# Splitting a two-key one-hot comparison into two operations with different layouts, in a PEER channel mixer

## The chip, the cores and the metric

The kernel runs on one core of one Trainium2 chip. The metric is the device time of one execution in microseconds; a kernel's time is the median of its runs.

## The reference

The reference is two layers of a diffusion backbone over 512 latent tokens and 256 context tokens, model width 1024. Each layer has a token mixer (global attention in layer 0, windowed attention in layer 1) and then a PEER channel mixer, which is where the change is:

```python
q = (hb @ w_q).reshape(n, PEER_HEADS, PEER_QDIM)          # 8 heads, 256
s1 = jnp.einsum('nhd,kd->nhk', q1, sub_keys[0])           # 128 first keys
s2 = jnp.einsum('nhd,kd->nhk', q2, sub_keys[1])           # 128 second keys
v1, i1 = lax.top_k(s1, PEER_TOPK)                         # 16 each
v2, i2 = lax.top_k(s2, PEER_TOPK)
cand_s = v1[..., :, None] + v2[..., None, :]
cand_i = i1[..., :, None] * N_KEYS + i2[..., None, :]
top_s, pos = lax.top_k(cand_s, PEER_TOPK)
expert = jnp.take_along_axis(cand_i, pos, axis=-1)        # one of 128 x 128 experts
g = jax.nn.softmax(top_s, axis=-1)
act = jax.nn.gelu(jnp.einsum('nhkd,nd->nhk', u_tab[expert], hb))
out = jnp.einsum('nhk,nhkd->nd', g * act, v_tab[expert])
```

So each token picks 8 x 16 = 128 experts, each named by a first key (0 to 127) and a second key (0 to 127), and gives each a gate `g`.

## The kernel before, in words

Two of the six 128-token tiles of layer 0, and one of the four of layer 1, gather the rows of their experts (`sparse_gen`, by indirect transfers that GpSimd issues). The other tiles, four latent tiles in layer 0 and three in layer 1, are computed densely: `dense` (L639) multiplies the tokens with all 16384 experts and weights the activations by a gate matrix that is zero wherever an expert was not picked. It goes through the first keys in order; five of them are worked ahead (`LEAD`), and from then on the loop alternates `outputs` and `weights`.

The gate matrix is made per tile by `build_g` (L526), which is called from the main loop (L825) right behind `topk_scan` and `topk_resolve` (L822, L823) of the same tile. `topk_resolve` leaves in a PSUM bank, for each token (on the free axis) and each of its 128 picks (on the partitions), the first key, the second key and the gate. L530 casts the two keys to bf16 into `ib` (128 x 2 x 128 tokens), L532 copies the gates into `gt`.

`build_g` then takes the 128 tokens of the tile in 16 groups of eight (`TB`), inside four blocks of 32 (`GB`). For a group:

- L551, VectorE: one comparison of `ib` with a table `iota_t` (made at L104 by GpSimd; it holds the key number, repeated eight times along the token axis) gives `hot`, bf16, for both keys at once. Its layout is (key kind, key 0 to 127, token 0 to 7): the token is innermost.
- L554, VectorE: `first` = the first key's half of `hot` times the gate, f32, in the layout (token, key). The read of `hot` is therefore stepped by eight elements, and the gate is repeated along the key axis.
- L557, ScalarE: `second` = the second key's half of `hot`, cast to f32 in the layout (token, key), with the same stepped read.
- L562, TensorE: for each token one matmul of `second` with `first` over the 128 picks gives that token's 128 x 128 gate matrix in PSUM (`gm`), four tokens to a bank.
- L541: the banks are copied to `gsb`, three of four by ScalarE, one by VectorE, one half group behind the matmuls (`LAG`). When 32 tokens are complete, a 2 MB transfer on SP's queue writes them to `Gd` in DRAM (L543, issued through the helper at L154). `dense` reads `Gd` back as `Gt`, which it waits for.

`hot` has two buffers, by alternating tags, one of each; `first`, `second` and `gsb` have two each.

Beside `build_g` other work is in the engines' queues: the modulation weights of layer 1 in three of layer 0's tiles (`ada_load` and `ada_cols`, L828), and the first `weights` of `dense` (L168 to L170, with ScalarE's cast at L160 and VectorE's subtraction at L162). The order within each engine's queue is set when the kernel is built, by a scheduler that goes by the order of the source as priority and by when an operation's inputs are ready in its own model; so independent operations can be moved past each other. In the trace of before, the comparisons of two groups stand next to each other ahead of the two `first`.

L488, L492, L506 and L507, which the prediction uses for durations, are small steps of `topk_resolve`: L492 multiplies the gates with a per-head factor that is repeated along the innermost axis, L506 combines two contiguous operands of the same size, and L507 reads what L506 wrote.

Of the kernel before, what the change touches and what calls it, by code (L numbers as in the profile page):

```python
# [12 lines left out]
BF16 = mybir.dt.bfloat16  # L13
U32 = mybir.dt.uint32
AF = mybir.ActivationFunctionType
ALU = mybir.AluOpType
# [4 lines left out]
P = 128  # L21
# [13 lines left out]
NK = 128  # L35
# [7 lines left out]
TB = 8  # L43
# [26 lines left out]
def body(ctx, tc, xT_in, cT_in, ada_w, ada_b, gains1, gains2, w_qkv, qk_gain, w_o, sinks,  # L70
         w_pq, subk, u_t, u_n, v_b, v_n, ropeC, ropeS, ropeR, out):
    nc = tc.nc
    V, A, G, T = nc.vector, nc.scalar, nc.gpsimd, nc.tensor

    const = ctx.enter_context(tc.tile_pool(name="const", bufs=1))
# [5 lines left out]
    def bank(tag, name, bufs):  # L81
        return ps.tile([P, 512], F32, tag=tag, name=name, bufs=bufs)
# [19 lines left out]
    V.memset(epst, EPS)  # L102
    iota_t = const.tile([P, NK, TB], BF16, name="iota_t")
    G.iota(iota_t, [[1, NK], [0, TB]], channel_multiplier=0, allow_small_or_imprecise_dtypes=True)  # L104
    ind = const.tile([P, NH + NKV, 16], F32, name="ind")
    V.memset(ind, 0.0)
    for h in range(NH + NKV):
# [41 lines left out]
    def nm(s):  # L149
        uid[0] += 1  # L150
        return f"{s}_{uid[0]}"

    def dma(dst, src):
        nc.sync.dma_start(dst, src)  # L154
# [371 lines left out]
    def build_g(pt, Gd, t, gp, kp):  # L526


        ib = gp.tile([P, 2, P], BF16, tag="ib", name=nm("ib"), bufs=2)
        A.copy(ib.rearrange("p a b -> p (a b)"), pt[:, :2 * P])  # L530
        gt = gp.tile([P, P], F32, tag="gt", name=nm("gt"), bufs=2)
        A.copy(gt, pt[:, 2 * P:3 * P])  # L532
        HT = TB // 2
        pending = []
        count = [0]

        def evacuate():
            po, gs, o, b = pending.pop(0)
            count[0] += 1
            eng = V.tensor_copy if count[0] % 4 == 0 else A.copy  # L540
            eng(gs[:, :, o:o + HT], po.rearrange("p (t a) -> p a t", t=HT))  # L541
            if o + HT == GB:
                dma(Gd[:, :, t * (P // GB) + b].rearrange("s p f -> p s f"),  # L543
                    gs.rearrange("p (s a) t -> p s (a t)", a=SC))

        for b in range(P // GB):
            gs = gp.tile([P, NK, GB], F32, tag="gsb", name=nm("gsb"), bufs=GSB)
            for n8 in range(GB // TB):
                tok = slice(b * GB + n8 * TB, b * GB + (n8 + 1) * TB)
                hot = kp.tile([P, 2, NK, TB], BF16, tag=("hot", "rep")[n8 % 2], name=nm("hot"), bufs=1)  # L550
                V.tensor_tensor(hot, iota_t[:, None].to_broadcast([P, 2, NK, TB]),  # L551
                                ib[:, :, None, tok].to_broadcast([P, 2, NK, TB]), ALU.is_equal)
                first = gp.tile([P, TB, NK], F32, tag="first", name=nm("first"), bufs=2)
                V.tensor_tensor(first, hot[:, 0].rearrange("p a t -> p t a"),  # L554
                                gt[:, tok, None].to_broadcast([P, TB, NK]), ALU.mult)
                second = gp.tile([P, TB, NK], F32, tag="second", name=nm("second"), bufs=2)
                A.copy(second, hot[:, 1].rearrange("p a t -> p t a"))  # L557
                for half in range(2):
                    po = bank("bg", nm("gm"), 4)
                    for i in range(HT):  # L560
                        k = half * HT + i
                        T.matmul(po[:, i * P:(i + 1) * P], second[:, k], first[:, k], start=True, stop=True)  # L562
                    pending.append((po, gs, (n8 * 2 + half) * HT, b))
                    if len(pending) > LAG:
                        evacuate()
        while pending:
            evacuate()
# [168 lines left out]
    for L in range(DEPTH):  # L736
# [83 lines left out]
        with pool(f"gp{L}") as gp:  # L820
            for t in range(c0 // P, NLAT // P):
                topk_scan(tk["l", t], v12["l", t], 1, kt)  # L822
                pt = topk_resolve(tk["l", t], i12["l", t], kt, "bg", lambda i, shape: kt.tile(  # L823
                    shape, BF16, tag=("hot", "rep")[i], name=nm("hot"), bufs=1))
                build_g(pt, Gd, t - c0 // P, gp, kt)  # L825
                if not last:
                    if t < 3:
                        ada_cols(1, mods[1], t, wp, ada_load(1, t, wp, 0))  # L828
# [4 lines left out]
        with pool(f"db{L}") as db:  # L833
            rb = rb_es.enter_context(pool(f"rb{L}", right=True))
            sg = groups[-1]["nm"]
            with pool(f"kc{L}") as kc:
                prep = []
                for t in stiles:
                    with later(SLACK2):
                        for hb in range(2):  # L840
                            topk_scan(tk[sg, t], v12[sg, t], hb, kc)
                        pt = topk_resolve(tk[sg, t], i12[sg, t], kc, "O", lambda i, shape: rb.tile(
                            shape, BF16, tag=("gu", "gv")[i], name=nm("hot"), bufs=(GUB, GVB)[i]))
# [90 lines left out]
```

## Time and profile before

| what | value |
|---|---|
| median of 3 runs | 4043.28 us (4041.41 to 4055.09) |
| the profiled execution | 4048.38 us, its span 4046.6 us |
| busy over the span: TensorE, its weight loads | 93%, 79% |
| busy over the span: VectorE, ScalarE, GpSimd | 76%, 38%, 25% |

The profiled execution is one run of the program with the hardware profiler on. Its span runs from the first to the last instruction; what lies around it makes up the rest of that run's own time. Shares of busy time are means over the span, and the stages have different limits, so the part of the span in which an edit lies has to be read by itself.

### The profile page before, as it was taken

To read this page: it belongs to the slowest core of one execution; us is meant where nothing else is said; L and a number is where in the kernel's file an instruction comes from. 1 tells how busy PE (TensorE), PEld (TensorE's weight loads), DVE (VectorE), ACT (ScalarE), POOL (GpSimd) and SP (SyncE) were. 2 spreads that over 40 slices of the span, in tenths; PEclk is the share of its full clock that TensorE was granted. 3 is DMA by queue.
4 is the path that set the end of the run, shared out by engine and by line. 5 is a ranking of instruction groups with operands and counts; after the bars stand their busy time and mean duration, and the time that the engine had idled before them with its cause. 6 is when DMAs were issued, how large, how long until landed. Compare 5 with 4: busy or idle time off the path is not lost.

```text
span 4046.6 us, 52056 instructions
## 1 busy us (share of the span) xinstructions
PE 3753.2 (93%) x19384; PEld 3200.5 (79%) x19384; DVE 3091.0 (76%) x5913; ACT 1536.2 (38%) x2217; POOL 1000.8 (25%) x778
## 2 busy tenths in 40 slices
PE   7999897768999999999999999998679999999999
PEld 5767685657877777787777867767678999999999
DVE  3373799986888888888888755579997877778775
ACT  3262316863222222222222233534873333333332
POOL 0000000001444554444454300000002444444420
PEclk9999998989999999999999999999999999999999
DMA  4303128665898899988888721121567888888874
GB/s 176 125 1 115 58 67 268 188 188 174 297 322 316 310 320 329 324 312 317 316 317 319 250 87 52 45 77 46 154 209 245 303 301 297 296 297 297 305 261 157
DMA packets 343407, 894.08 MB, mean 221 GB/s; under 512 B 25968, under 2 KB 145904, under 8 KB 338800
## 3 DMA queue, kind: packets, MB, share of 16 engines
q1 hardware_dynamic: 232560, 488.05, 35.2%
q0 software_dynamic: 110592, 402.70, 28.6%
q8 instruction: 152, 2.49, 0.2%
q14 instruction: 103, 0.84, 0.1%
HBM read 826.16 MB, written 64.49 MB: 220 GB/s over the span
## 4 chain that ended last, share of the span: by engine, by line
PE 49%; issue 19%; DVE 13%; DMA 10%; POOL 8%; ACT 2%; POOLq 0%; SPq 0%; DVEq 0%; ACTq 0%
PE sp L170 5%; DMA gv<-v_n,idx 5%; PE sp L168 5%; PE sp L169 5%; DVE first L554 4%; POOL gv L598 4%; POOL gu L598 4%; PE pj L168 4%; PE pj L169 4%; PE pj L170 4%; DMA gu<-u_n,idx 3%; PE kp L682 2%; PE kp L683 2%; PE kp L681 2%; PE op L683 2%
## 5 line engine op out<-in xcount | busy, mean ns | idle before, releaser
L598 POOL DMA_INDIRECT gu<-u_n,idx x384 | 548.8, 1429 | 2670.0 <-DVE idx L578 964.3
L168 PE MATMUL sp<-hil,Uh 128*128 128x512 f32 (+1 forms) x2048 | 750.8, 367 | 29.8 <-ACT act L659 29.5
L169 PE MATMUL sp<-lol,Uh 128*128 128x512 f32 (+1 forms) x2048 | 751.2, 367 | 0.0
L170 PE MATMUL sp<-hil,Ul 128*128 128x512 f32 (+1 forms) x2048 | 747.0, 365 | 2.6 <-DVE Ul L162 2.6
L626 DVE SCALAR_TENSOR_TENSOR acc<-gv,w,acc 128x1024 f32<-128x1024 f32 x381 | 489.5, 1285 | 138.3 <-DMA gv<-v_n,idx 137.6
L667 ACT CAST wh<-act 128x512 fp32r<-128x512 f32 (+1 forms) x256 | 145.0, 567 | 1039.9 <-DVE act L665 1033.3
L598 POOL DMA_INDIRECT gv<-v_n,idx x384 | 448.9, 1169 | 330.8 <-DVE acc L626 220.2
L616 DVE CUSTOM_DVE_ANT_0 gu<-gu,hn 128x1024 f32<-128x1024 f32 x384 | 468.0, 1219 | 66.7 <-DMA gu<-u_n,idx 66.6
L168 PEld LDWEIGHTS sp<-hil,Uh 128*128 128x128 f32 x2048 | 387.4, 189 | 75.9 <-ACT act L659 30.2
L162 DVE TENSOR_TENSOR Ul<-Ur,Uh 128x1024 fp32r<-128x1024 f32 x256 | 312.4, 1221 | 170.8 <-ACT Uh L160 170.7
L682 PE MATMUL kp<-wh,Vl 128*128 128x512 f32 (+1 forms) x1024 | 381.9, 373 | 47.5 <-DVE Vl L162 47.2
L170 PEld LDWEIGHTS sp<-hil,Ul 128*128 128x128 f32 x2048 | 387.3, 189 | 47.1 <-DVE Ul L162 3.9
L169 PEld LDWEIGHTS sp<-lol,Uh 128*128 128x128 f32 x2048 | 387.6, 189 | 38.5
L160 ACT CAST Uh<-Ur 128x1024 fp32r<-128x1024 f32 x256 | 269.0, 1051 | 391.2 <-PE sp L169 384.5
L681 PE MATMUL kp<-wh,Vh 128*128 128x512 f32 (+1 forms) x1024 | 378.5, 370 | 0.8 <-ACT wh L667 0.7
L683 PE MATMUL kp<-wl,Vh 128*128 128x512 f32 (+1 forms) x1024 | 379.1, 370 | 0.0
L681 PE MATMUL op<-wh,Vh 128*128 128x512 f32 (+1 forms) x1024 | 371.3, 363 | 0.6 <-DVE xl L652 0.6
L683 PE MATMUL op<-wl,Vh 128*128 128x512 f32 (+1 forms) x1024 | 370.8, 362 | 0.0
L682 PE MATMUL op<-wh,Vl 128*128 128x512 f32 (+1 forms) x1024 | 370.7, 362 | 0.0
L160 ACT CAST Vh<-Vr 128x1024 fp32r<-128x1024 f32 x256 | 268.7, 1050 | 221.0 <-PE op L683 201.8
L562 PE MATMUL gm<-first,second 128*128 128x128 f32 x1792 | 239.9, 292 | 98.0 <-DVE first L554 88.1
L562 PEld LDWEIGHTS gm<-first,second 128*128 128x128 f32 x1792 | 223.9, 204 | 126.8 <-ACT second L557 79.3
(228 smaller groups left out, 6660.3 us busy)
## 6 DMA issues: line engine op xcount, KB each, us to landing
Ur<-u_t SPq DMA_DIRECT2D x256, 512.0 KB, 6.0
Vr<-v_b SPq DMA_DIRECT2D x256, 512.0 KB, 6.8
Gd<-gsb SPq DMA_DIRECT2D x28, 2048.0 KB, 9.1
Gt<-Gd SPq DMA_DIRECT2D x32, 1024.0 KB, 8.1
Gt<-Gd SPq DMA_DIRECT2D x32, 768.0 KB, 7.1
ar<-ada_w SPq DMA_DIRECT2D x32, 512.0 KB, 10.3
wr<-ada_w SPq DMA_DIRECT2D x32, 512.0 KB, 4.6
wr<-w_pq SPq DMA_DIRECT2D x32, 512.0 KB, 3.5
```

The costliest lines, as they stand in the source:

```text
L160: A.copy(hi, raw)
L162: V.tensor_tensor(lo, raw, hi, ALU.subtract)
L168: T.matmul(o, sh, mh, start=i == 0, stop=False)
L169: T.matmul(o, sh, ml, start=False, stop=False)
L170: T.matmul(o, sl, mh, start=False, stop=i == n - 1)
L562: T.matmul(po[:, i * P:(i + 1) * P], second[:, k], first[:, k], start=True, stop=True)
L598: G.indirect_dma_start(out=r, out_offset=None, in_=tab, in_offset=bass.IndirectOffsetOnAxis(ap=idx[:, s:s + 1], axis=0))
L616: V.tensor_tensor_reduce(out=r, in0=r, in1=hn, scale=1.0, scalar=0.0, op0=ALU.mult, op1=ALU.add, accum_out=sd[:, k:k + 1])
L626: V.scalar_tensor_tensor(acc[ti], r, w[:, k:k + 1], acc[ti], ALU.mult, ALU.add)
L681: T.matmul(o[:, :n], vh[:, k, ds], wh, start=start, stop=False, skip_group_check=True)
L682: T.matmul(o[:, :n], vl[:, k, ds], wh, start=False, stop=False, skip_group_check=True)
L683: T.matmul(o[:, :n], vh[:, k, ds], wl, start=False, stop=stop, skip_group_check=True)
```

## The change

The comparison of L551 becomes two. The first key's is written with the key innermost, the layout in which `first` is multiplied and written, against a second table `iota_a` in which the key number runs along the innermost axis; `ib` is repeated along that axis. The second key's keeps the token innermost, and `second` is read from it as before. Buffers, tags, matmuls, copies and transfers are unchanged; the comparison of the second key stands behind the multiplication in the source.

```diff
     iota_t = const.tile([P, NK, TB], BF16, name="iota_t")
     G.iota(iota_t, [[1, NK], [0, TB]], channel_multiplier=0, allow_small_or_imprecise_dtypes=True)
+    iota_a = const.tile([P, TB, NK], BF16, name="iota_a")
+    G.iota(iota_a, [[0, TB], [1, NK]], channel_multiplier=0, allow_small_or_imprecise_dtypes=True)
...
-                hot = kp.tile([P, 2, NK, TB], BF16, tag=("hot", "rep")[n8 % 2], name=nm("hot"), bufs=1)
-                V.tensor_tensor(hot, iota_t[:, None].to_broadcast([P, 2, NK, TB]),
-                                ib[:, :, None, tok].to_broadcast([P, 2, NK, TB]), ALU.is_equal)
+                hot = kp.tile([P, 2, TB * NK], BF16, tag=("hot", "rep")[n8 % 2], name=nm("hot"), bufs=1)
+                rows = hot[:, 0].rearrange("p (t a) -> p t a", t=TB)
+                cols = hot[:, 1].rearrange("p (a t) -> p a t", t=TB)
+                V.tensor_tensor(rows, iota_a, ib[:, 0, tok, None].to_broadcast([P, TB, NK]), ALU.is_equal)
                 first = gp.tile([P, TB, NK], F32, tag="first", name=nm("first"), bufs=2)
-                V.tensor_tensor(first, hot[:, 0].rearrange("p a t -> p t a"),
-                                gt[:, tok, None].to_broadcast([P, TB, NK]), ALU.mult)
+                V.tensor_tensor(first, rows, gt[:, tok, None].to_broadcast([P, TB, NK]), ALU.mult)
+                V.tensor_tensor(cols, iota_t, ib[:, 1, None, tok].to_broadcast([P, NK, TB]), ALU.is_equal)
                 second = gp.tile([P, TB, NK], F32, tag="second", name=nm("second"), bufs=2)
-                A.copy(second, hot[:, 1].rearrange("p a t -> p t a"))
+                A.copy(second, cols.rearrange("p a t -> p t a"))
```

## Rows read from the trace of the kernel before

**Rows 1.** The page: busy us (share) of each engine; shares of the chain, by line.
```profile
PE 3753.2 (93%) x19384; PEld 3200.5 (79%) x19384; DVE 3091.0 (76%) x5913; ACT 1536.2 (38%) x2217; POOL 1000.8 (25%) x778
...
PE sp L170 5%; DMA gv<-v_n,idx 5%; PE sp L168 5%; PE sp L169 5%; DVE first L554 4%; POOL gv L598 4%; POOL gu L598 4%; PE pj L168 4%; PE pj L169 4%; PE pj L170 4%; DMA gu<-u_n,idx 3%; PE kp L682 2%; PE kp L683 2%; PE kp L681 2%; PE op L683 2%
```

**Rows 2.** Windows, the seven stretches of build_g: length, busy us, clock, DMA share, GB/s.
```profile
625.50:679.40 53.90, 42.80 (x310) 32.32 (x300) 53.39 (x41) 44.18 (x39) 0.00 (x0) 0.94 0.77 237
...
2938.30:2991.30 53.00, 39.42 (x284) 36.19 (x282) 52.96 (x40) 46.06 (x45) 0.00 (x0) 0.97 0.47 136
sum 372.70, PE 273.81 PEld 235.74 DVE 371.66 ACT 314.31 POOL 0.00; mean PE 39.12 PEld 33.68 DVE 53.09 ACT 44.90 POOL 0.00
```

**Rows 3.** Waits, 2871 to 2938 us: total us, times, longest.
```profile
PE gm L562 <- DVE first L554: 17.9, 14, 2.1
PEld gm L562 <- ACT second L557: 13.5, 6, 2.3
```

**Rows 4.** Groups of instructions, build_g's lines: busy us, mean ns of one; idle before.
```profile
L557 ACT CAST second<-hot 128x1024 f32<-128x1024 bf16 x112 | 226.4, 2060 | 12.8 <-DVE hot L551 12.8
L554 DVE TENSOR_TENSOR first<-hot,gt 128x1024 f32<-128x1024 bf16 x112 | 225.4, 2018 | 0.0
L551 DVE TENSOR_TENSOR hot<-iota_t,ib 128x2048 bf16<-128x2048 bf16 x112 | 132.6, 1234 | 1.7 <-ACT ib L530 1.7
```

**Rows 5.** Timeline of VectorE, one period: start us, us.
```profile
726.16 2.34 DVE L551 TENSOR_TENSOR hot<-iota_t,ib 128x2048 bf16<-128x2048 bf16 x2
728.43 2.02 DVE L554 TENSOR_TENSOR first<-hot,gt 128x1024 f32<-128x1024 bf16 x1
730.37 0.67 DVE L541 COPY gsb<-gm 128x512 f32<-128x512 f32 x1
730.97 2.00 DVE L554 TENSOR_TENSOR first<-hot,gt 128x1024 f32<-128x1024 bf16 x1
732.89 2.34 DVE L551 TENSOR_TENSOR hot<-iota_t,ib 128x2048 bf16<-128x2048 bf16 x2
```

**Rows 6.** Reference durations: two groups (mean ns), two lines (ns min/median/max).
```profile
L162 DVE TENSOR_TENSOR Ul<-Ur,Uh 128x1024 fp32r<-128x1024 f32 x256 | 312.4, 1221 | 170.8 <-ACT Uh L160 170.7
L160 ACT CAST Uh<-Ur 128x1024 fp32r<-128x1024 f32 x256 | 269.0, 1051 | 391.2 <-PE sp L169 384.5 <-DMA Ur<-u_t 3.1 <-issue 2.3
L492 DVE TENSOR_TENSOR ts<-ts,gs x10: 278/283/286, 617.8 to 3032.0; 128x128 f32<-128x128 f32 x10
L506 DVE TENSOR_TENSOR low<-c,low x10: 275/291/294, 617.6 to 3031.8; 128x128 uint32<-128x128 uint32 x10
```

**Rows 7.** Timeline of ScalarE, the same period; in brackets the idle time before.
```profile
728.02 4.04 ACT L557 CAST second<-hot 128x1024 f32<-128x1024 bf16 x2
731.96 1.28 ACT L541 COPY gsb<-gm 128x512 f32<-128x512 f32 x2
734.28 0.59 ACT L541 COPY gsb<-gm 128x512 f32<-128x512 f32 x1 [1.05 <-PE gm L562]
734.76 2.04 ACT L557 CAST second<-hot 128x1024 f32<-128x1024 bf16 x1
```

**Rows 8.** Chain in order of time, behind the last stretch of each layer.
```profile
881.17 10.14 DMA Gd<-gsb
...
2994.34 10.47 DMA Gd<-gsb
3004.89 5.85 DMA Gt<-Gd
```

**Rows 9.** GpSimd's table at the start: ns min/median/max.
```profile
L104 POOL IOTA iota_t<- x1: 1607/1607/1607, 1.6 to 1.6; 128x1024 bf16 x1
```

**Rows 10.** Timeline of VectorE: an instruction and the reader of its output.
```profile
2928.86 0.29 DVE L506 TENSOR_TENSOR low<-c,low 128x128 uint32<-128x128 uint32 x1
2929.19 0.29 DVE L507 TENSOR_TENSOR low<-low,pos 128x128 uint32<-128x128 uint32 x1
```

## The prediction

> **What bounds the kernel now.** I read the page's busy shares and its chain first, then the table of the stretches in which the one-hot work runs, then who waits there, then the instructions of one period. Over the span TensorE is the busy engine (93%), but an average over stages does not price this edit: the chain names `first` (L554) with 4% of the span, the largest share of any VectorE line [rows 1]. The edit sits in `build_g`, which runs seven times, four in layer 0 and three in layer 1, each time 16 groups of eight tokens, 112 groups in all. In these seven stretches, 372.7 us together, VectorE is busy for 371.7 us, ScalarE for 314.3 and TensorE for 273.8 [rows 2]. There is no hole in VectorE. The others wait for it: in the sixth stretch TensorE's `gm` matmuls wait 17.9 us for `first`, and 13.5 us for ScalarE's `second` before their weight loads [rows 3]. So inside `build_g` a microsecond off VectorE is a microsecond off the time, until ScalarE is full.
>
> One period of the steady pattern holds two groups: two `hot` compares, `first`, a copy of `gsb`, `first`, and the next `hot` starts 6.73 us after the last pair [rows 5]. An instruction's slot (start to next start) is its duration less about 0.08 us: the 2.02 us `first` holds 1.94 [rows 5]. The slots are 2.27 for two `hot`, 1.94 and 1.92 for the two `first`, 0.60 for the copy. 56 periods of 6.73 us make 377 us, which agrees with the 372.7 of the stretches (each begins without the copy).
>
> **The change, part by part.** *Removed:* per group one compare over 2 x 1024 elements, 1.234 us, slot 1.135, and a `first` whose bf16 operand is read with a step of eight elements, 2.018 us, slot 1.93 [rows 4, 5]. Together 3.065 us a group.
>
> *`first` with a contiguous operand.* Why does it take 2.018 us for 1024 elements? Two suspects: the stepped read of `hot`, and `gt`, which is repeated along the innermost axis. L492 has an operand repeated just so and takes 283 ns for 128 elements; L506, of the same size without it, takes 291 [rows 6]: the repetition is free. The stepped read also shows on ScalarE, where `second` takes 2060 ns [rows 4] and a contiguous cast of the same size 1051 [rows 6]. So I blame the step, and take L162, two contiguous inputs and 1024 f32 out: 1.22 us, slot 1.14 [rows 6]. Lower bound: the same, since `gt` and the output are f32. Upper bound: nothing gained, slot 1.93, if the mix of bf16 in and f32 out is the slow part; no row shows that mix contiguous.
>
> *The second key's compare* keeps its shape with half the elements. L506 and L162 differ by 896 elements and 0.93 us, so an f32 pass costs 1.04 ns an element and 0.16 us fixed [rows 6]; `hot` then ran at (1.234 - 0.16)/2048 = 0.52 ns, two elements a cycle of the f32 pass [rows 4]. Half of it is 0.16 + 1024 x 0.52 = 0.69 us, slot 0.61.
>
> *The first key's compare* now repeats `ib` along the innermost axis. No row shows a 16-bit compare with that pattern. Bounds: 0.61 if it keeps two elements a pass, 1.14 if it falls to one, like L162. The nearest rows in access pattern are those with an innermost repeat, L492 and `first` itself, and none of them beats one element a pass [rows 4, 6]; I take 1.14. The Trainium skill ("VectorE: DVE Perf Modes", What auto-detection actually checks) speaks against this change here: the packed mode wants every tensor 16-bit with a step of one, and a step of zero is not one. By it the compare costs 1.14; were the rule not to hold, the sum below would be 59 us better for VectorE. No run so far shows which.
>
> *Sum on VectorE:* 1.14 + 1.14 + 0.61 = 2.89 against 3.065 a group, 0.175 less; x 112 = 19.6 us. The period falls to 6.38.
>
> *ScalarE and the place of `second`.* `second` itself is untouched (same stepped read, 2.06 us), but it now waits for the compare that comes last in the source, behind `first`, where it used to start behind the shared compare. Its input is ready 1.75 us after the group's start if the queue puts the second compare ahead of `first`, 2.89 if it keeps the source's order; before it was 1.135 [rows 5]. What is queued behind it on ScalarE are the `gsb` copies, and TensorE waits for both. A ScalarE period is two `second` (3.94 us to the next start), a first copy of some 0.6, the wait of 1.05 for TensorE's half group, and the copy that follows, 0.48: 6.1 us [rows 7]. That is under 6.38, so VectorE stays the limit, by 0.3 us only. At the end of a stretch nothing covers the shift: the last `second` ends 2.06 us behind its compare, and this is 0.9 to 2.1 us behind the last `first`, which was the later one before. Between two stretches VectorE has other work; behind the last stretch of each layer the write of `Gd` and all that follows wait: 2 x 1 to 2 us, I take 3 in all.
>
> *Does the gain reach the end?* Behind each layer's last stretch the chain runs straight on: 10.14 us of `Gd` in layer 0, 10.47 in layer 1 and then 5.85 of `Gt` [rows 8]. Layer 0 has 4 x 16 groups, 11.2 us; layer 1 has 3 x 16, 8.4 us. I take off nothing more there. The DMA share of the first stretch, 0.77, rises with the shorter period to 0.77 x 6.73/6.38 = 0.81 [rows 2, 5], and a `Gd` block has two periods, 12.8 us, to land in its 10.14.
>
> *Edits costed at nothing.* The new table is one more iota on GpSimd, 1.6 us at the start of the program like L104 [rows 9]; behind it on that queue stand the two masks, which only layer 1's attention reads. If that cover were gone it would cost the 1.6 us once. No DMA moves, and nothing passes SP's queue.
>
> *Total:* -19.6 + 3 = -16.6 us. The profiled execution took 4048.4 us (span 4046.6), so 4031.8; it stands 5.1 above the median of the runs, 4043.3, so the forecast for the median is 4026.7, about 4027 (-0.4%). Some 0.3%, 12 us, is what a measurement of this kernel can tell from no change.
>
> **Rivals.**
> *The gain is eaten by waits; no change.* VectorE never waited for itself because two independent compares stood between a compare and its `first`. If the queue holds compare and `first` side by side, the reader waits for the writer: L507, which reads L506's output, starts 0.33 us after it, where 0.21 is the slot of its 0.29 us [rows 10], so 0.12 x 112 = 13 us back. ScalarE's 6.1 us against 6.38 may slip as well: 0.3 us a period is 17 us. For it: the small margin. Against it: the queue as written before kept dependent pairs apart. Time 4035 to 4047.
>
> *Slower: `first` does not speed up.* If not the step but the mix of types makes `first` slow, three instructions cost 1.14 + 1.93 + 0.61 = 3.68 against 3.065: +0.615 x 112 = +69 us, 4112. The kernel turns slower once the new `first` holds a slot above 1.315. Against it: ScalarE's doubling on the same read. For it: no contiguous read of this mix exists in the trace.
>
> *Faster than forecast: the first compare stays packed.* VectorE's period falls to 2 x 2.36 + 0.60 = 5.32, and ScalarE's 6.1 becomes the bound: 56 x (6.73 - 6.1) = 35 us, 4008; if ScalarE's waits close up too, its busy share (314.3 of 372.7) is the floor, 58 us at most, 3985.
>
> That the change doesn't do what it says is the second rival: the contiguous read is its one saving.
>
> **How the numbers follow.** Forecast 0.52 (4020 to 4034, about nine tenths of it over 0.3% faster), eaten gain 0.26 (mostly within 0.3%), slower 0.13, packed 0.09. Faster: 0.47 + 0.01 + 0.09 = 0.57; same: 0.05 + 0.24 = 0.29; slower: 0.13 + 0.01 = 0.14. The range runs from 4004, which takes in the packed case where ScalarE bounds it, to 4052; outside are the slower case and a packed case that goes further.
>
> **What would show it.** After: L554 at 1.22 us; two compare lines of 112 instructions, near 1.22 and 0.69; `second` still 2.06; a period near 6.4 with VectorE full. Wrong if the first compare shows 0.69, if L554 stays near 2.0, or if VectorE shows idle time for ScalarE or TensorE inside the stretches.

## The result and the profile after

The changed kernel takes **4182.1 us** (median of five runs, 4175.8 to 4198.2) against 4044.5 us for the kernel before (five runs beside them): a ratio of 1.0341, 95% interval 1.0327 to 1.0355. It is slower by 138 us, where 17 us less were forecast. The profiled execution of after is the slowest of its five, 4198.2 us with a span of 4196.4; against the span of before, 4046.6, that is 149.8 us more.

The groups of the one-hot work, after: line, engine, operation, tiles, count, then busy time and mean ns of one, then the idle time of the engine ahead of them and what ended it (L555 is the first key's compare, L557 `first`, L558 the second key's compare, L560 `second`, L565 `gm`, L543 the copies).

```profile
L555 DVE TENSOR_TENSOR hot<-iota_a,ib 128x1024 bf16<-128x1024 bf16 x112 | 136.4, 1218 | 4.4 <-ACT ib L532 4.4
L557 DVE TENSOR_TENSOR first<-hot,gt 128x1024 f32<-128x1024 bf16 x112 | 136.6, 1220 | 0.1
L558 DVE TENSOR_TENSOR hot<-iota_t,ib 128x1024 bf16<-128x1024 bf16 x112 | 76.8, 686 | 0.0
L560 ACT CAST second<-hot 128x1024 f32<-128x1024 bf16 x112 | 227.1, 2028 | 6.1 <-DVE hot L558 6.1
L565 PE MATMUL gm<-first,second 128*128 128x128 f32 x1792 | 304.2, 339 | 180.7 <-ACT second L560 179.9 <-DVE hot L555 0.8
L543 ACT COPY gsb<-gm 128x512 f32<-128x512 f32 x168 | 98.4, 586 | 183.9 <-PE gm L565 183.9
L543 DVE COPY gsb<-gm 128x512 f32<-128x512 f32 x56 | 38.7, 692 | 160.9 <-PE gm L565 160.9
```

The matmuls and the copies before, in the same view:

```profile
L562 PE MATMUL gm<-first,second 128*128 128x128 f32 x1792 | 239.9, 292 | 98.0 <-DVE first L554 88.1 <-DVE gsb L541 4.8 <-ACT second L557 3.4
L541 ACT COPY gsb<-gm 128x512 f32<-128x512 f32 x168 | 97.3, 593 | 43.7 <-PE gm L562 41.7
L541 DVE COPY gsb<-gm 128x512 f32<-128x512 f32 x56 | 39.2, 699 | 1.4 <-PE gm L562 1.4
```

The two compares, `first` and `second` took what was forecast: 1.22, 0.69, 1.22 and 2.03 us against 1.22, 0.69, 1.22 and 2.06. None of the four is to blame. The last column tells where the time went: ScalarE's copies wait 183.9 us in all for TensorE (41.7 before), TensorE's matmuls wait 179.9 us for ScalarE's `second` (3.4 before), and VectorE, which waited 1.4 us in front of its copies before, stands idle there for 160.9 us. Two engines that wait for each other take turns; they don't overlap.

The seven stretches, from a tile's first compare to the end of its last `first` (the view by windows: length, busy time with count of PE, PEld, DVE, ACT, POOL, then TensorE's granted clock, DMA share, GB/s). The first, the fifth, the seventh and the sum, to be laid beside [rows 2]:

```profile
627.50:692.40 64.90, 45.09 (x326) 30.71 (x318) 50.84 (x57) 42.74 (x38) 0.00 (x0) 0.97 0.77 245
...
2883.80:2959.70 75.90, 48.86 (x248) 44.27 (x246) 50.92 (x56) 43.66 (x43) 0.00 (x0) 0.71 0.29 83
...
3066.40:3134.60 68.20, 45.02 (x284) 41.04 (x282) 50.93 (x56) 44.39 (x42) 0.00 (x0) 0.87 0.35 101
sum 491.20, PE 325.96 PEld 279.07 DVE 356.08 ACT 306.65 POOL 0.00; mean PE 46.57 PEld 39.87 DVE 50.87 ACT 43.81 POOL 0.00
```

491.2 us against 372.7: 118.5 of the 149.8 us are inside the stretches, although VectorE's work in them fell from 371.7 to 356.1. Another 17.7 lie between them: the five gaps inside the layers add up to 85.6 us against 67.9, because behind the last `first` more matmuls and copies are still to come (a stretch's last copy ends 4.7 to 7.6 us behind its last `first`, before 2.9 to 4.3). The remaining 14 us lie ahead of the first stretch (2), between the two layers (5) and behind the last stretch (7). The granted clock tells a second story: 0.71 in the fifth stretch, where the seven stretches of before have 0.89 to 0.98 (the first and the last of them in [rows 2]). The first stretch of after kept 0.97, and it is the shortest, 64.9 us.

One period of two groups on ScalarE, after, at full clock (start, duration, instruction, and in brackets the idle time before it and who ended it):

```profile
733.49 2.02 ACT L560 CAST second<-hot 128x1024 f32<-128x1024 bf16 x1
736.75 0.59 ACT L543 COPY gsb<-gm 128x512 f32<-128x512 f32 x1 [1.25 <-PE gm L565]
737.65 0.59 ACT L543 COPY gsb<-gm 128x512 f32<-128x512 f32 x1 [0.31 <-PE gm L565]
738.13 2.03 ACT L560 CAST second<-hot 128x1024 f32<-128x1024 bf16 x1
741.41 0.59 ACT L543 COPY gsb<-gm 128x512 f32<-128x512 f32 x1 [1.25 <-PE gm L565]
741.89 2.02 ACT L560 CAST second<-hot 128x1024 f32<-128x1024 bf16 x1
```

Between two `second` there is always a copy that waits 1.25 us, the time of TensorE's half group, and TensorE's half group could start only when the `second` ahead of the copy was done. Before, two `second` ran back to back ahead of the copies [rows 7]. ScalarE's queue in the fifth stretch, from its start, shows it for three builds, the third of which ("cols first") is the first experiment below (s2 is the `second` of group 2, c2.1 and c2.2 ScalarE's copies of its first and second half; VectorE takes every fourth copy):

```
before          s0 s1 c0.1 c0.2 s2 c1.1 s3 c2.1 c2.2 c3.1 s4 s5 c4.1 c4.2 c5.1 s6 s7 c6.1 ...
after           s0 c0.1 s1 c0.2 c1.1 s2 c2.1 c2.2 s3 c3.1 s4 c4.1 c4.2 s5 c5.1 s6 ...
cols first      s0 s1 c0.1 c0.2 s2 c1.1 s3 c2.1 c2.2 s4 c3.1 s5 c4.1 c4.2 s6 ...
```

Before, the `second` of group n+1 stands ahead of the first copy of group n in 72 of the 105 pairs of the seven stretches, for every even n among them; where it stands behind it, two `second` follow each other (c5.1 s6 s7 c6.1), so that ScalarE waits once in two groups. After, it stands behind it in 104 of 105. ScalarE does not go past such a copy to a `second` whose input is ready. The `second` at 741.89 reads this compare, done at 739.20:

```profile
738.51 0.69 DVE L558 TENSOR_TENSOR hot<-iota_t,ib 128x1024 bf16<-128x1024 bf16 x1
```

Even so ScalarE stood still from 740.16 to 741.41 in front of the copy. So it can't begin the next `second` until TensorE has done half of this group, and TensorE has no `gm` matmuls to do until that `second` is done. The period is 8.40 us (733.49 to 741.89), where it was 6.73 [rows 5].

The same in the fifth stretch, where the period is 10.33:

```profile
2940.44 2.01 ACT L560 CAST second<-hot 128x1024 f32<-128x1024 bf16 x1
2944.06 0.59 ACT L543 COPY gsb<-gm 128x512 f32<-128x512 f32 x1 [1.61 <-PE gm L565]
2944.54 2.01 ACT L560 CAST second<-hot 128x1024 f32<-128x1024 bf16 x1
2948.72 0.59 ACT L543 COPY gsb<-gm 128x512 f32<-128x512 f32 x1 [2.17 <-PE gm L565]
2950.29 0.59 ACT L543 COPY gsb<-gm 128x512 f32<-128x512 f32 x1 [0.98 <-PE gm L565]
2950.77 2.02 ACT L560 CAST second<-hot 128x1024 f32<-128x1024 bf16 x1
```

The order is the same, the waits for TensorE are longer: 1.61, 2.17 and 0.98 instead of 1.25, 1.25 and 0.31. VectorE, meanwhile, waits 3.98 us in front of one copy:

```profile
2945.76 0.69 DVE L543 COPY gsb<-gm 128x512 f32<-128x512 f32 x1 [3.98 <-PE gm L565]
```

Within one stretch both speeds occur. Two windows of the seventh (columns as above):

```profile
3079.00:3096.00 17.00, 10.64 (x81) 9.62 (x80) 13.01 (x15) 12.53 (x13) 0.00 (x0) 1.00 0.44 124
3103.00:3124.00 21.00, 13.91 (x64) 12.87 (x64) 13.02 (x15) 11.31 (x11) 0.00 (x0) 0.66 0.35 100
```

At a granted clock of 1.00 the period is 8.43 us, at a mean of 0.66 it is 10.41. Read in pieces of 2 us, the clock goes back and forth inside a period between its two levels, 2.4 GHz (granted 1.00) and 1.2 GHz (0.50). The 16 `gm` matmul instructions of a group take 2.05 us at the upper level and up to 3.79 at the lower one.

### The profile page after: what moved, and what is told of

It reads as the page before. It is cut to its first block, busy times and chain, and to the rows that moved or that the text cites. A ratio compares the mean times of both kernels' runs of the same rounds, so it can differ in the third digit from the quotient of the medians.

```text
span 4196.4 us, 52118 instructions
## 1 busy us (share of the span) xinstructions
PE 3823.7 (91%) x19384; PEld 3257.1 (78%) x19384; DVE 3076.2 (73%) x6025; ACT 1540.0 (37%) x2217; POOL 995.8 (24%) x779
## 4 chain that ended last, share of the span: by engine, by line
PE 49%; issue 18%; DVE 10%; DMA 10%; POOL 7%; ACT 7%; POOLq 0%; SPq 0%; ACTq 0%; DVEq 0%
DMA gv<-v_n,idx 5%; PE gm L565 5%; ACT second L560 5%; PE sp L170 5%; PE sp L172 5%; PE sp L171 5%; POOL gu L601 4%; POOL gv L601 3%; PE pj L170 3%; PE pj L172 3%; PE pj L171 3%; DMA gu<-u_n,idx 3%; PE kp L684 2%; PE kp L686 2%; PE kp L685 2%
## 5 line engine op out<-in xcount | busy, mean ns | idle before, releaser
L619 DVE CUSTOM_DVE_ANT_0 gu<-gu,hn 128x1024 f32<-128x1024 f32 x384 | 468.3, 1220 | 73.3 <-DMA gu<-u_n,idx 73.0
L565 PE MATMUL gm<-first,second 128*128 128x128 f32 x1792 | 304.2, 339 | 180.7 <-ACT second L560 179.9
L565 PEld LDWEIGHTS gm<-first,second 128*128 128x128 f32 x1792 | 277.7, 244 | 223.1 <-ACT second L560 220.8
```

The costliest lines, as they stand in the source:

```text
L619: V.tensor_tensor_reduce(out=r, in0=r, in1=hn, scale=1.0, scalar=0.0, op0=ALU.mult, op1=ALU.add, accum_out=sd[:, k:k + 1])
```

## The experiments

The theory from here on: the loss is the place of `second` in ScalarE's queue (copy n.1 ahead of `second` n+1), made worse by a lower TensorE clock while TensorE waits. Rivals: the new layout of `hot` harms somewhere unseen; the copies' lag behind the matmuls is too short; the clock is only a bystander.

### The second key first in the source

```diff
+                V.tensor_tensor(cols, iota_t, ib[:, 1, None, tok]...)
+                second = gp.tile(...)
+                A.copy(second, cols.rearrange("p a t -> p t a"))
                 V.tensor_tensor(rows, iota_a, ib[:, 0, tok, None]...)
                 first = gp.tile(...)
                 V.tensor_tensor(first, rows, gt[:, tok, None]...)
-                V.tensor_tensor(cols, iota_t, ib[:, 1, None, tok]...)
-                second = gp.tile(...)
-                A.copy(second, cols.rearrange("p a t -> p t a"))
```

> The changed kernel with its source lines in another order: second key's compare and `second` first, then the first key's compare and `first`. Same operations; as built, ScalarE's queue then has `second` of group n+1 ahead of the first copy of group n, where the changed kernel has it behind. Queue-order theory (ScalarE's copy, placed ahead of the next `second`, waits for TensorE, which waits for `second`): the period of two groups falls from 8.4 to 10.4 us to about 6.4, time about 4025 to 4035, a little under the kernel before. Rival 'VectorE's copy blocks VectorE' (its place in VectorE's queue behind two groups' work is almost unchanged): stays near 4180. Rival 'the new layouts themselves slow the stretch': stays near 4180.

4031.2 us (4027.2 to 4039.4) against 4048.0 for before in the same job: a ratio of 0.9957, interval 0.9941 to 0.9974. The same operations, in another order of the source, are 151 us faster than after and 17 us faster than before. VectorE has no holes in a period from the steady part (here L555 is the second key's compare, L558 the first key's, L560 `first`):

```profile
775.47 1.22 DVE L558 TENSOR_TENSOR hot<-iota_a,ib 128x1024 bf16<-128x1024 bf16 x1
776.60 0.69 DVE L555 TENSOR_TENSOR hot<-iota_t,ib 128x1024 bf16<-128x1024 bf16 x1
777.20 1.22 DVE L560 TENSOR_TENSOR first<-hot,gt 128x1024 f32<-128x1024 bf16 x1
...
781.21 0.68 DVE L543 COPY gsb<-gm 128x512 f32<-128x512 f32 x1
781.81 1.21 DVE L558 TENSOR_TENSOR hot<-iota_a,ib 128x1024 bf16<-128x1024 bf16 x1
```

The period, 775.47 to 781.81, is 6.34 us; the forecast for the change was 6.38. The sum over the seven stretches:

```profile
sum 362.82, PE 267.84 PEld 227.50 DVE 355.60 ACT 323.21 POOL 0.00; mean PE 38.26 PEld 32.50 DVE 50.80 ACT 46.17 POOL 0.00
```

That is 9.9 us less than the 372.7 of before, with VectorE 16.1 us less busy and idle for 7 us. So 10 of the 17 us gained lie inside the stretches. Of the rest, 4 lie ahead of the first stretch and 3 behind the last, and nothing here ties those to the change. The layout is not what harms: with the better queue the steady period is the one that its instructions promise. ScalarE's queue has `second` one group ahead again, as the list above shows.

### Forcing ScalarE's order alone

```diff
-LAG = 1
+LAG = 2
-                A.copy(second, cols.rearrange("p a t -> p t a"))
+                sec = A.copy(second, cols.rearrange("p a t -> p t a"))
...
                     if len(pending) > LAG:
-                        evacuate()
+                        with tc.issue_after(sec.ins):
+                            evacuate()
```

and, as its control, the longer lag without the forced order:

```diff
-LAG = 1
+LAG = 2
```

> The changed kernel, compares in its own source order, with LAG 2 and the copies queued on ScalarE behind the newest `second` (issue order only); VectorE's queue as built is the same as in the changed kernel. Queue-order theory: as e1, 4025 to 4040 (the second compare is ready later, so perhaps 5 to 10 us over e1). Rival 'VectorE's copy blocks VectorE': stays near 4180, since that queue is untouched. Rival 'layouts': stays near 4180.

> Control for e2: the changed kernel with LAG 2 alone. As built, ScalarE still alternates `second` of group n, first copy of group n. Queue-order theory: no gain, 4165 to 4200. Were it LAG and not the order that helps in e2, this would come down to e2's time.

Forced: 4058.4 us (ten runs, 4050.1 to 4071.3), ratio 1.0026, interval 1.0015 to 1.0038. Lag alone: 4171.2 us in one run, where before took 4048.0. So 124 of the 138 us come back with the forced order and the longer lag together. The lag alone brings 11 in one run, 5 us under the fastest run of after, and its queue on ScalarE has copy n.1 ahead of `second` n+1 in 102 of 105 pairs. The order itself is thus worth some 113 to 124 us. The forced version stays 27 us behind the version with the second key first, and its waits say where:

```profile
PE gm L565 <- ACT second L560: 110.8, 84, 3.0
ACT second L560 <- DVE hot L558: 76.8, 55, 2.9
```

(Who waits, for whom: us in all, how often, the longest.) VectorE's queue of compares, `first` and copies is that of after, instruction for instruction, so the other rival of the expectations, that VectorE's own copy does the harm, is out as the main cause. But the second key's compare is still late in it, and the copy can stand in front of that compare; `second` then waits up to 2.9 us for its input. The forecast of 4025 to 4040 missed this: the place of the producer counts in both queues.

### The same order with the old operations

In the kernel of before, each `second` is ordered behind ScalarE's last copy traced before it; nothing else is changed. The lines added, shortened:

```diff
+            done = eng(gs[:, :, o:o + HT], ...)
+            if eng == A.copy:
+                last[0] = done
...
+                with tc.issue_after(last[0].ins) if last[0] is not None else nullcontext():
                     A.copy(second, hot[:, 1].rearrange("p a t -> p t a"))
```

> The kernel before, one compare and the stepped read kept, with each `second` queued on ScalarE behind the last copy traced before it, so that ScalarE alternates `second` n, first copy n, `second` n+1 as in the changed kernel. Queue-order theory: the loss appears without the split, period 8.4 us or more, time 4140 to 4220. Rival 'layouts' and rival 'VectorE's copy': near 4045.

4100.9 us in one run, 53 more than before: the loss appears without the change's operations, but at two fifths of its size, under the range expected. ScalarE's timeline shows why (L561 is `second`, L542 the copy here):

```profile
2867.93 0.58 ACT L542 COPY gsb<-gm 128x512 f32<-128x512 f32 x1 [1.25 <-PE gm L566]
2868.41 2.03 ACT L561 CAST second<-hot 128x1024 f32<-128x1024 bf16 x1
2870.34 0.57 ACT L542 COPY gsb<-gm 128x512 f32<-128x512 f32 x1
2871.68 0.58 ACT L542 COPY gsb<-gm 128x512 f32<-128x512 f32 x1 [0.77 <-PE gm L566]
2872.16 2.01 ACT L561 CAST second<-hot 128x1024 f32<-128x1024 bf16 x1
2875.42 0.58 ACT L542 COPY gsb<-gm 128x512 f32<-128x512 f32 x1 [1.25 <-PE gm L566]
```

The period is 7.49 us (2867.93 to 2875.42): here the copy of a second half stands behind the next `second`, not ahead of it, so one group's turn is shorter than in after. 56 x (7.49 - 6.73) = 43 of the 53 us, and the seven stretches together are 48 us longer than before. After, both of ScalarE's copies of an even group stand ahead of the next `second`, and the period is 8.4.

### The split with the old layout

The first key's compare and `first` get the old layout back (token innermost, stepped read); the split and the order of the source stay.

```diff
-                rows = hot[:, 0].rearrange("p (t a) -> p t a", t=TB)
-                V.tensor_tensor(rows, iota_a, ib[:, 0, tok, None]..., ALU.is_equal)
-                V.tensor_tensor(first, rows, gt[:, tok, None]..., ALU.mult)
+                rows = hot[:, 0].rearrange("p (a t) -> p a t", t=TB)
+                V.tensor_tensor(rows, iota_t, ib[:, 0, None, tok]..., ALU.is_equal)
+                V.tensor_tensor(first, rows.rearrange("p a t -> p t a"), gt[:, tok, None]..., ALU.mult)
```

> The changed kernel's split and source order, but the first key's compare in the old layout (token innermost, no second table) and `first` with the stepped read. VectorE's period is then two of 0.61 + 0.61 + 1.93 and a copy, 6.9 us. As built, ScalarE's order is mixed: about half of the seconds stand ahead of the previous group's first copy, half behind. Queue-order theory: between, 4070 to 4150. If the contiguous layout itself did the harm: about 4055, 10 us of VectorE's added work and no more.

4081.8 us in one run (before 4045.1): slower than before by 37 us with the layout undone. ScalarE's queue in this build mixes both orders. It agrees with the queue theory without proving it: the durations on VectorE differ from after's too.

### The clock

Does the lower clock cost time, or does it only accompany the waits? Three versions with ScalarE strictly taking turns (each `second` ordered behind the last copy as above, and `LAG = 0`), without and with matmuls that nobody reads, put behind each group's own. The fillers are added work, and no output changes. The lines for the lag and for the narrow fillers, of 128 columns:

```diff
-LAG = 1
+LAG = 0
...
+                    if half == 1:
+                        with tc.issue_after(mm.ins):
+                            idle = bank("O", nm("idle"), 2)
+                            for i in range(FILL):
+                                T.matmul(idle[:, :P], ident, second[:, 0], start=True, stop=True)
```

A first series (none, five of 512 columns, ten of 128) had by an oversight another lag, that of the query and key projection, set from 1 to 0 too.

> The changed kernel with ScalarE's order written out by hand: LAG 0 and each `second` queued behind the last copy traced before it, so as built `second` n, copies of n, `second` n+1 everywhere (nearly the order of the changed kernel). Queue-order theory: same as the changed kernel, 4165 to 4200, with periods of 8.4 us where TensorE's granted clock is 1.00 and about 10.4 where it is 0.66. It is the base for e6.

> e5 with five 128x512 matmuls of identity and `second` behind each group's `gm` matmuls, into a bank that nobody reads: work added, 560 matmuls, no output changed. ScalarE's order as built is e5's. If part of the loss is the lower TensorE clock that follows from TensorE standing idle in the alternation: the clock stays near 1.00 in the stretches, every period is about 8.4 us, and the time falls to 4120 to 4160 although work is added. If the long periods have another cause (VectorE's copies, memory): no gain, or 10 to 100 us slower by the added matmuls.

> e6 again with a filler that fits: ten 128x128 matmuls of identity and `second` behind each group's `gm` matmuls (about 1.25 us at full clock; TensorE stands idle for about 2.1 us a group in e5), 1120 matmuls added, their bank read by nobody. e6's five 128x512 f32 matmuls took 4.3 us a group and made TensorE the bound, so it told nothing of the clock. Clock theory: granted clock near 1.00 in all stretches, period about 8.4 us throughout, time 4140 to 4185 against e5's 4210, though work is added. Rival (the long periods have another cause): 4210 or slower, with periods of 10 us at full clock.

Without fillers 4209.9 us (ratio 1.0401, interval 1.0375 to 1.0427), a little above the range. The five wide ones gave 4379.0 (1.0827, 1.0809 to 1.0845): a test that failed, since they alone took 4.5 us of TensorE a group (500.1 us in 112 groups, in the row at the end of this document) and made TensorE the bound. The ten narrow ones gave 4204.2 (1.0375, 1.0348 to 1.0403), above the 4140 to 4185 expected: in layer 1 the clock stayed at 0.97 to 1.00 and the period at 8.7 us instead of up to 10.4, but the time hardly moved, because TensorE was late with other work between layer 0's third and fourth stretch (48 us apart instead of 16). The second series has the projection's lag as in after, and a version with five narrow ones.

> The kernel of after in strict lock-step as before (each second ordered behind the copy traced before it, no lag of the gm copies), but with the lag of the query and key projection left as in the kernel of after: in lock0 and in its two filled versions that lag had also been set from 1 to 0, which has nothing to do with the one-hot work. If that second edit is what made lock0 slower than after, this run takes 4175 to 4190 us; if the stricter order itself costs it, 4200 to 4215. In layer 1's three stretches the clock theory expects periods of 8.4 us at their start and about 10.4 later, some 209 us from first to last compare of the three, as in lock0.

> The same with ten unread 128-column matmuls a group added. Clock theory: TensorE stays at full clock in layer 1's stretches, the period is 8.7 us throughout and the three take about 185 us from first to last compare, against 209 without the fillers. Rival (the copies and queues alone set the period, not the clock): the three take as long as without fillers or longer, since the fillers add 2.4 us of TensorE work a group. Whole time: 15 to 25 us under the run without fillers if nothing else moves; no difference if work of other stages is pushed back by the fillers in layer 0 again.

> The same with five unread matmuls a group. Clock theory: if five keep the engine at full clock the period is 8.4 to 8.6 us and layer 1's three stretches take 180 to 187 us; if the clock still falls in part, between 187 and 209. Rival as above: 209 or more. Less filler displaces less in layer 0, so the whole time should be 10 to 30 us under the run without fillers.

| matmuls added a group | median us (range) | ratio to before, 95% | layer 1's three stretches, us |
|---|---|---|---|
| none | 4210.9 (4201.0 to 4216.3) | 1.0408 (1.0390 to 1.0425) | 222.7 |
| five | 4142.2 (4140.3 to 4154.7) | 1.0232 (1.0215 to 1.0249) | 196.0 |
| ten | 4198.3 (4195.0 to 4203.2) | 1.0374 (1.0356 to 1.0391) | 197.1 |

4210.9 against 4209.9: the projection's lag had no part in it. And with five useless matmuls a group **added**, the kernel becomes 69 us faster (the two profiled executions, the fastest without fillers and the slowest with five, are 46 us apart, and the seven stretches of the two 49). Layer 1's last stretch without fillers, then with five (columns as in the windows above):

```profile
3065.90:3140.10 74.20, 51.42 (x281) 47.08 (x280) 50.92 (x56) 44.44 (x42) 0.00 (x0) 0.75 0.33 93
```

```profile
3025.70:3090.70 65.00, 52.87 (x419) 49.01 (x418) 50.83 (x56) 44.83 (x42) 0.00 (x0) 1.00 0.39 109
```

419 matmul instructions in about the busy time of 281, at a clock of 1.00 instead of 0.75. ScalarE's waits for TensorE in the late part of such a stretch, without fillers:

```profile
3103.61 0.58 ACT L544 COPY gsb<-gm 128x512 f32<-128x512 f32 x1 [2.17 <-PE gm L569]
...
3108.27 0.59 ACT L544 COPY gsb<-gm 128x512 f32<-128x512 f32 x1 [2.17 <-PE gm L569]
3109.98 0.58 ACT L544 COPY gsb<-gm 128x512 f32<-128x512 f32 x1 [1.12 <-PE gm L569]
```

and with five fillers:

```profile
3064.66 0.58 ACT L545 COPY gsb<-gm 128x512 f32<-128x512 f32 x1 [1.25 <-PE gm L570]
3065.55 0.58 ACT L545 COPY gsb<-gm 128x512 f32<-128x512 f32 x1 [0.31 <-PE gm L570]
3066.04 2.04 ACT L565 CAST second<-hot 128x1024 f32<-128x1024 bf16 x1
3069.33 0.59 ACT L545 COPY gsb<-gm 128x512 f32<-128x512 f32 x1 [1.25 <-PE gm L570]
```

The waits are 1.25 and 0.31 again, those of after at full clock. The rival, that the clock is a bystander, expected the stretches to stay or grow. The range expected for five fillers, 180 to 187 us from the first to the last compare, just holds by the first key's compares: 63.1 + 60.9 + 62.1 = 186.1 (by the second key's it is 188.8). With none it is 213.7, where 209 were expected, with ten 184.7, as expected. The whole time fell by more than the 10 to 30 us expected: that range reckoned with work pushed back in layer 0, and the fourth stretch there starts 14 us behind the third's last `first`, as it should.

What each step costs, then, as periods of two groups: 6.73 us before; 7.49 where ScalarE and TensorE take turns in half of each group's copies; 8.4 where they do so in all that ScalarE copies; 10.4 where TensorE's clock falls as well. For the 118.5 us inside after's stretches I estimate the split from the version with five fillers, whose seven stretches, from first compare to end of last `first` in its timeline, take 455.5 us: 455.5 - 372.7 = 83 us for the order and 491.2 - 455.5 = 36 us for the clock. After's own first stretch, at 0.97, leads to the same without fillers: 7 x 64.9 = 454 us.

## Why the prediction was wrong

**The durations and VectorE's sum were right.** All four operations came within 0.04 us. The second key first in the source gives the forecast period (6.34 against 6.38) and a gain of 17 us, the size forecast, though it was forecast for the other order of the lines. In part that is luck: only 10 of the 17 lie inside the stretches, where 19.6 were forecast.

**The repeated first-key compare falls to one element a pass**, as taken: 1218 ns against 686 for the packed one with as many elements. The Trainium skill ("VectorE: DVE Perf Modes", What auto-detection actually checks) asks for a step of one in every tensor of the packed mode, which a step of zero is not, and the trace agrees. The packed rival is out.

**The stepped read was the cause of the 2.02 us**: `first` runs in 1220 ns once its read is contiguous, with bf16 in and f32 out as before. The slower rival rested on the opposite and is out; the kernel is slower for a reason that stood in no rival.

**The step that failed** is "A ScalarE period is two `second` [...], a first copy of some 0.6, the wait of 1.05 for TensorE's half group, and the copy that follows, 0.48: 6.1 us [rows 7]. That is under 6.38, so VectorE stays the limit". It summed ScalarE's period over the queue of before, with two `second` in a row, and so with one wait for TensorE per period. The build of after has a copy between any two `second`, with three waits per period (1.25, 0.31, 1.25), and ScalarE's loop is 8.4 us. The sum also left out a copy: [rows 7] show three a period, 1.28 for two and 0.48 for the third, and 3.94 + 1.28 + 1.05 + 0.48 is 6.75, which is over 6.38. That 6.34 was reached all the same with the second key first shows that the wait of 1.05 was no fixed price. ScalarE there does two `second` and three copies without a wait in 5.37 us (775.49 to 780.86):

```profile
775.49 0.64 ACT L543 COPY gsb<-gm 128x512 f32<-128x512 f32 x1
775.96 2.13 ACT L557 CAST second<-hot 128x1024 f32<-128x1024 bf16 x1
777.93 1.14 ACT L543 COPY gsb<-gm 128x512 f32<-128x512 f32 x2
778.88 2.15 ACT L557 CAST second<-hot 128x1024 f32<-128x1024 bf16 x1
780.86 0.66 ACT L543 COPY gsb<-gm 128x512 f32<-128x512 f32 x1
```

The paragraph did ask what was queued behind `second`, and did note that its input comes last in the source; it then moved its start time and left its place in the queue. That was the error: the order is made from the source when the kernel is built, and the change moved `second`'s producer behind `first` in the source.

**The first rival named the danger and argued it away.** "The queue as written before kept dependent pairs apart" was read from VectorE's queue alone, and from a queue that the change would build anew. ScalarE's margin of 0.3 us a period was called small, and its slip priced at 17 us; the price of the copy going ahead of `second` could be worked out from [rows 7]: two `second` (3.94), two turns of 1.05 plus 0.6, and the third copy, 0.48: 7.7 us a period, some 55 us over the seven stretches against a VectorE period of 6.73. That would have made a slower rival of the right mechanism, though still too small.

**The clock** stands in [rows 2] (0.94 and 0.97), and the sum has no term for it: it was put at nothing without a reason. It fell to 0.71 to 0.87 in six of the seven stretches, while TensorE waited in every group, and cost some 36 us more by the estimate above.

**What would show it** was stated rightly: "Wrong [...] if VectorE shows idle time for ScalarE or TensorE inside the stretches". It shows 160.9 us.

**Open** is why the builder puts copy n.1 ahead of `second` n+1 after the change. That it follows from the order of the lines is shown, by the version that only swaps them; by which times in the builder's own model it comes about was not looked into. That a lag of two does not change it is shown by one run.

## What to carry to other kernels

Price a reordered source by the queues that it will build, not by durations alone: wherever an engine both makes the input of the next engine and takes away that engine's result, ask whether the next input stands ahead of the wait for the last result. If it doesn't, the two engines take turns, and a microsecond saved elsewhere is worth nothing, as VectorE's 15.6 us were here (371.7 to 356.1). So put the producer that starts the longest chain of other engines (here the second key's compare, which ScalarE and then TensorE wait for) first in the source.

## What the runs showed of the hardware

- TensorE's granted clock fell where TensorE waited in every group: 0.71 to 0.87 over layer 1's stretches of after, down to its lower level, 1.2 GHz, inside a period. There the wait for a half group is 2.17 us instead of 1.25, so a stall makes the next stall longer. Waiting alone did not always bring it down: the first stretch of after kept 0.97 in the same order, and the kernel of before with its order forced 0.97 to 1.00 in layer 1, at a period of 7.49 us; what decides between them is not shown. Five unread matmuls a group kept the clock at 0.97 to 1.00 in layer 1 and made that kernel 69 us faster; ten lost most of that again in layer 0, whose third and fourth stretch then lay 48 us apart instead of 14.
- An f32 matmul of `gm` or of the fillers stands in these traces as two instructions: 8 tokens in 112 groups are 896 `gm` matmuls, and the row counts 1792. The five 512-column fillers cost twice their number for that reason:

```profile
L575 PE MATMUL idle<-second,ident 128*128 128x512 f32 x1120 | 500.1, 593 | 0.0
```

560 matmuls in the source, 1120 in the row.
